# A two-layer hybrid diffusion step on one core: the builder's scheduler orders the instructions by its timeline model

## The chip, the cores and the metric

The kernel runs on one core of one Trainium2 chip. The core's engines are TensorE (PE, matmuls), VectorE (DVE), ScalarE (ACT), GpSimd (POOL) and SyncE (SP, which issues most DMAs). Each takes its own list of instructions strictly in order and waits by semaphores for the others. The metric is the device time of one execution in microseconds (us); lower is better.

## The reference

Two layers over 128 context tokens and 512 latent tokens, D = 1024, in float32; the same weights for both groups, with shifts, scales and gates from each group's conditioning vector.

```
def _layer(x, mod, shared, cached):
    shift1, scale1, gate1, shift2, scale2, gate2 = jnp.split(mod, 6, axis=-1)
    proj = (x * (1 + scale1) + shift1) @ w_in
    ...
    o_rwkv, s_f, s_b = _rwkv_mix(f_rwkv, s0, s0, rwkv_p)
    o_na = _neighbourhood_attention(na_q, na_k, na_v, na_k_ctx, na_v_ctx, rpb)
    ...
    o_g = _blocked_attention(g_q.reshape(b, n, H_GQA_KV, GQA_GROUP, HEAD_DIM), keys, vals)
    ...
    mix = jnp.concatenate([o_rwkv, o_na, o_g], -1) @ w_out
    x = _layer_norm(DEEPNORM_ALPHA * x + gate1 * mix, ln1_w, ln1_b)
    gate, up = jnp.split((x * (1 + scale2) + shift2) @ w_ffn_in, 2, axis=-1)
    x = _layer_norm(DEEPNORM_ALPHA * x + gate2 * ((jax.nn.silu(gate) * up) @ w_ffn_out), ln2_w, ln2_b)
```

`mod` is SiLU(cond) @ w_mod + b_mod. `_rwkv_mix` is a scan over the tokens, forward and backward, in 4 heads of 64 (RWKV-7); the neighbourhood attention has 4 heads on a grid of 8 x 64, with a learned bias; GQA has 8 query and 2 key heads. The outputs are the tokens of both groups, the scan's final states and the context's keys and values.

## The kernel before

The 640 tokens stand in the free dimension, in two halves of 320 columns. Weights arrive as float32 by DMA (`wraw`, L306, two buffers), and `split` makes of each a high and a low part: ACT casts the high one (`whi`, L277), DVE subtracts (`wlo`, L278). `mm3` then issues three matmuls for each block of 128 x 128 (high by high, high by low, low by high). All matmuls pass through one line, L72, transposes through L76, so groups are told apart by their tiles: `ps_s`, `ps_rw` and `ps_pv` are the three kinds of PSUM tiles.

The start (`first_input`) contracts 1024 = 8 x 128 in steps `k`. Each step needs the block `x{k}` of the input (L371) and its scale and shift. These come from `w_modT` (L186, multiplied and summed on DVE, L194) for all scales and for the first two shifts; the other six shifts come from rows of `w_mod` (L203) through matmuls into `ps_pv`, from `cst`, made from `c_raw` through a SiLU (L163). Later modulation values come through `ps_pv` as well.

Each layer has eight jobs of the scan. A job works on chunks of 64 tokens and needs inverses of 64 x 64 triangular matrices: PE's products go to DRAM (`md`), come back as blocks of 16 x 16 (`BT`, L723), DVE inverts the blocks, these go to DRAM (`td`, `xd`, issued by ACT) and come back as 64 x 64 matrices (`T`, L797; `X`, L799), and PE finishes the inverse and forms the states. While a job is between those DMAs, the kernel runs units of the two attentions: keys and queries come from DRAM (`ks`, L962, three buffers; `qs`, L955), the bias (`bias`, L948) and values (`vw`, L938) too. Then follow `w_out`, layer norm (sums `lnS`, `lnQ`), and the feed-forward part.

What sets the order: the program is written as generators. `spawn`, `tick` and `weave` take the next piece of a job when a hand-kept clock (`Tensor.now`, which adds an estimate per matmul) says that it is ready, and so write one sequence. The tile framework's scheduler then goes through it with a model of when each instruction is ready, and appends to each engine's list the ready instruction of the highest priority; priority follows the written sequence, except where `high_priority` moves one (L306's split by 50 places, for example). The model says only in what order instructions are listed; on the chip semaphores decide when they run. Buffers are reused in the listed order, so a load may wait for the last reader of its buffer, and what stands behind it on SP waits too.

The function that the diff touches builds and runs the program:

## Time and profile before

| | |
|---|---|
| median of 3 runs | 2181.78 us (2178.21 to 2183.61) |
| profiled execution, its time | 2182.43 us |
| its span | 2180.7 us, 41209 instructions |
| mean granted clock of PE | 0.965 |
| busy: PE, DVE, ACT, POOL | 94%, 60%, 42%, 9% |
| DMA | 226.46 MB, mean 104 GB/s |

The profile is one execution. Rows of it are times in us from the span's start. PE's matmul and weight loads overlap, and the granted clock is a share of full speed, so a low clock makes matmuls longer without idle time. An idle engine costs nothing by itself: what counts is which wait ends last in each stretch.

### The profile page before, as it was taken

The numbers are of one execution on the slowest core, as the hardware profiler recorded it, in microseconds if no ns is written. First come the engines' busy times: TensorE is split into PE (matmuls) and PEld (weight loads), VectorE is DVE, ScalarE is ACT, GpSimd is POOL, SyncE is SP. The second block draws the span as 40 slices with busy tenths as digits, with TensorE's granted clock in tenths as the row PEclk, the third lists the DMA queues.
The fourth block names the chain that finished last, engine by engine and source line by source line (L and its number), as shares of the span: only waits on it lengthen the run. The fifth ranks groups of instructions, "written<-read, shape, count | busy, mean of one in ns | idle before, by whom it ended". The sixth has DMA issues, their size and how long they took to land.

```text
span 2180.7 us, 41209 instructions
## 1 busy us (share of the span) xinstructions
PE 2052.8 (94%) x16737; PEld 1861.4 (85%) x16737; DVE 1302.1 (60%) x2874; ACT 909.8 (42%) x1823; POOL 189.8 (9%) x355
## 2 busy tenths in 40 slices
PE   6989989799999999999999997879999999999997
PEld 4876867577889999999988886658779999999997
DVE  6445676586776666666765666567767533323247
ACT  3434455465663212212365445356555521221234
POOL 0001131010100000000020223011101000000000
PEclk9999998799999999999999999789999999999998
DMA  8554344211424444444442425241014222222223
GB/s 295 147 161 159 108 94 95 49 34 29 142 73 136 145 155 151 148 139 151 141 133 69 130 69 110 54 94 27 23 48 139 65 69 78 69 73 83 75 84 112
DMA packets 186597, 226.46 MB, mean 104 GB/s; under 512 B 119062, under 2 KB 128918, under 8 KB 186278
## 3 DMA queue, kind: packets, MB, share of 16 engines
q1 hardware_dynamic: 150148, 206.72, 32.3%
q0 software_dynamic: 3984, 11.90, 1.7%
q10 hardware_dynamic: 32274, 5.20, 1.4%
q8 instruction: 132, 2.16, 0.4%
q14 instruction: 59, 0.48, 0.1%
HBM read 198.37 MB, written 25.40 MB: 103 GB/s over the span
## 4 chain that ended last, share of the span: by engine, by line
PE 80%; DMA 8%; DVE 5%; ACT 3%; issue 3%; SPq 1%; POOL 0%; ACTq 0%; DVEq 0%; POOLq 0%
PE ps_s L72 43%; PE ps_rw L72 29%; PE ps_pv L72 5%; PE ps_rw L76 4%; DMA td<-TB 3%; DMA T<-td 1%; DMA wmod<-in_w_mod 1%; ACT whi L277 1%; DMA BT<-md 1%; DVE wlo L278 0%; DMA xa<-in_xT 0%; ACT prob L1127 0%; DMA c_raw<-in_cT 0%; PE ps_s L76 0%; DMA md<-X 0%
## 5 line engine op out<-in xcount | busy, mean ns | idle before, releaser
L72 PE MATMUL ps_s<-xh,whi 128*128 128x320 f32 x1312 | 417.9, 321 | 24.2 <-ACT xh L277 11.6
L72 PE MATMUL ps_s<-xh,wlo 128*128 128x320 f32 x1312 | 409.9, 313 | 2.5 <-DVE wlo L278 2.5
L72 PE MATMUL ps_s<-xl,whi 128*128 128x320 f32 x1312 | 410.0, 313 | 0.6 <-DVE xl L278 0.4
L72 PEld LDWEIGHTS ps_s<-xh,whi 128*128 128x128 f32 x1312 | 249.1, 190 | 46.9 <-ACT xh L277 13.7
L72 PEld LDWEIGHTS ps_s<-xh,wlo 128*128 128x128 f32 x1312 | 249.4, 190 | 6.9 <-DVE wlo L278 4.4
L72 PEld LDWEIGHTS ps_s<-xl,whi 128*128 128x128 f32 x1312 | 249.8, 190 | 5.5 <-issue 2.9
L278 DVE TENSOR_TENSOR wlo<-wraw,whi 128x1024 fp32r<-128x1024 f32 (+1 forms) x118 | 141.4, 1199 | 159.9 <-ACT whi L277 159.2
L72 PE MATMUL ps_s<-xh,flo 128*128 128x320 f32 x736 | 228.7, 311 | 0.0
L72 PE MATMUL ps_s<-xl,fhi 128*128 128x320 f32 x736 | 228.5, 310 | 0.0
L72 PE MATMUL ps_s<-xh,fhi 128*128 128x320 f32 x736 | 228.4, 310 | 0.0
L277 ACT CAST whi<-wraw 128x1024 fp32r<-128x1024 f32 (+1 forms) x118 | 121.1, 1027 | 250.7 <-PE ps_s L72 146.6
L277 ACT CAST fhi<-wraw 128x1024 fp32r<-128x1024 f32 (+1 forms) x82 | 83.3, 1016 | 206.3 <-PE ps_s L72 99.8
L72 PEld LDWEIGHTS ps_s<-xh,fhi 128*128 128x128 f32 x736 | 138.9, 189 | 0.1
L72 PEld LDWEIGHTS ps_s<-xh,flo 128*128 128x128 f32 x736 | 138.8, 189 | 0.1
L72 PEld LDWEIGHTS ps_s<-xl,fhi 128*128 128x128 f32 x736 | 138.9, 189 | 0.0
L278 DVE TENSOR_TENSOR flo<-wraw,fhi 128x1024 fp32r<-128x1024 f32 (+1 forms) x82 | 97.0, 1184 | 57.7 <-ACT fhi L277 57.6
L72 PE MATMUL ps_s<-ks,qs 128*128 128x256 f32 (+1 forms) x384 | 102.4, 373 | 24.9 <-DMA qs<-nqd 15.4
L1431 ACT ACTIVATE sg<-ps_s 128x320 f32<-128x320 f32 x88 | 38.2, 435 | 189.1 <-PE ps_s L72 189.0
L1432 DVE TENSOR_TENSOR sg<-sg,ps_s 128x320 f32<-128x320 f32 x88 | 42.8, 486 | 120.1 <-ACT sg L1431 119.8
L1278 DVE SCALAR_TENSOR_TENSOR z<-ps_rw,modT,z 128x128 f32<-128x128 f32 (+2 forms) x144 | 59.0, 436 | 90.0 <-PE ps_rw L72 89.8
L72 PE MATMUL ps_rw<-hh,flo 128*128 128x320 f32 x352 | 109.7, 312 | 0.6 <-DVE flo L278 0.6
L72 PE MATMUL ps_rw<-hh,fhi 128*128 128x320 f32 x352 | 109.5, 311 | 0.0
(397 smaller groups left out, 4482.1 us busy)
## 6 DMA issues: line engine op xcount, KB each, us to landing
wraw<-in_w_ffn_in SPq DMA_DIRECT2D x88, 512.0 KB
wmod<-in_w_modT SPq DMA_DIRECT2D x66, 512.0 KB
wraw<-in_w_in_f SPq DMA_DIRECT2D x42, 512.0 KB
wraw<-in_w_ffn_out SPq DMA_DIRECT2D x48, 448.0 KB
wmod<-in_w_mod SPq DMA_DIRECT2D x48, 256.0 KB
wraw<-in_w_out SPq DMA_DIRECT2D x16, 512.0 KB
wraw<-in_w_ffn_out SPq DMA_DIRECT2D x16, 512.0 KB
ks<-nkd SPq DMA_DIRECT2D x16, 384.0 KB
```

The costliest lines, as they stand in the source:

```text
L72: self.eng.matmul(out, lhsT, rhs, **kw)
L76: self.eng.transpose(out, src, ident)
L277: self.nc.scalar.copy(hi, src)
L278: self.nc.vector.tensor_tensor(lo, src, self.r32(hi), ALU.subtract)
L1278: nc.vector.scalar_tensor_tensor(z[:, a:b], ps[:, q], g, xa[:, q], ALU.mult, ALU.add)
L1431: nc.scalar.activation(sg, pg, AF.Silu)
L1432: nc.vector.tensor_tensor(sg, sg, pu, ALU.mult)
```

## The change

One argument of the tile framework's context. With it, the scheduler takes its timeline model in place of the default model to decide when instructions are ready, and so which is listed next. Instructions, tiles, buffers and shapes are those of before; there is one table load fewer on ACT.

```
-    with tile.TileContext(nc) as tc:
+    with tile.TileContext(nc, schedule_with_timeline_sim=True) as tc:
         Build(tc, I, O).run()
```

The lists change on all engines. Three places follow; numbers behind a name tell tiles of one kind apart, and names without one are inputs in DRAM if they begin with `in_`.

SP at the start, from the ninth DMA on, before (`wmod` are modulation weights, `x2` to `x7` blocks of the input, `wraw` weights of the projection, `rp` the bias table):

```order
L306 DMA wraw_144<-in_w_in_f 128x1024
L306 DMA wraw_150<-in_w_in_f 128x1024
L186 DMA wmod_163<-in_w_modT 128x1024
L203 DMA wmod_172<-in_w_mod 128x768
L203 DMA wmod_176<-in_w_mod 128x768
L203 DMA wmod_180<-in_w_mod 128x768
L371 DMA x2_186<-in_xT 128x640
L371 DMA x3_248<-in_xT 128x640
L203 DMA wmod_184<-in_w_mod 128x768
```

And now:

```order
L186 DMA wmod_163<-in_w_modT 128x1024
L203 DMA wmod_172<-in_w_mod 128x768
L371 DMA x2_186<-in_xT 128x640
L371 DMA x3_248<-in_xT 128x640
L371 DMA x4_284<-in_xT 128x640
L371 DMA x5_337<-in_xT 128x640
L371 DMA x6_376<-in_xT 128x640
L371 DMA x7_415<-in_xT 128x640
L203 DMA wmod_602<-in_w_mod 128x512
L306 DMA wraw_144<-in_w_in_f 128x1024
L203 DMA wmod_618<-in_w_mod 128x512
L916 DMA rp_1052<-in_rpb 60x31
```

All blocks of the input and `wmod_602` moved ahead of `wraw_144`, and the rows `wmod_176` to `wmod_184` behind `rp_1052`.

ACT near the end of the scan's feature stage, before (`cx`, `f`, `rt`, `FT`, `BK` and `RHO` are features of the scan; `whi_1131` is the high part of the attention's first query weights):

```order
L524 COPY cx_960<-ps_s2_927 128x320
L670 ACTIVATE rt30_1204<-rt30_1204 128x320
L528 ACTIVATE f8_995<-cx_960,pp0_103 128x512
L672 ACTIVATE rt00_1225<-rt20_1173 128x320
L673 ACTIVATE rt20_1173<-rt20_1173 128x320
L535 ACTIVATE rt10_1172<-ps_rw_1178,hbias_1068 128x320
L535 ACTIVATE f8_995<-f8_995 128x640
L732 COPY RHO0_1492<-FT0_1222 128x320
L684 COPY BK0_1223<-BK0_1223 64x5x64
L277 CAST whi_1131<-wraw_1133 128x1024
L277 CAST whi_1234<-wraw_1236 128x1024
L988 ACTIVATE nqc_1125<-ps_s2_1137 128x128
```

And now, the place at which `whi_1131` stands:

```order
L210 COPY wmod_784<-ps_pv_601 64x256
L277 CAST whi_921<-wraw_923 128x1024
L524 COPY cx_786<-ps_s2_757 128x320
L528 ACTIVATE f4_829<-cx_786,pp0_103 128x512
L277 CAST whi_1131<-wraw_1133 128x1024
L524 COPY cx_875<-ps_s2_842 128x320
L562 ACTIVATE kksq_1085<-kk1_1083 128x640
L678 COPY FT0_1222<-f4_829 128x5x64
L678 COPY FT1_1786<-f4_829 128x5x64
L528 ACTIVATE f5_914<-cx_875,pp0_103 128x512
```

The cast moved from behind the features' decay and key tiles to a place ahead of `cx_875`, 22 rows up.

SP in layer 1, at the second pair of heads of the neighbourhood attention, before (`nkd1`, `nqd1` hold its keys and queries, `gkd1`, `gqd1` those of GQA, `md` a product of the scan):

```order
L962 DMA ks_15155<-nkd1_12541 64x2x768 x2
L955 DMA qs_15161<-nqd1_12540 128x1x512
L955 DMA qs_15163<-nqd1_12540 128x1x512
L723 DMA BT1_14794<-md_14632 40x16x16
L962 DMA ks_15158<-nkd1_12541 64x2x768
L948 DMA bias_15128<-rpx1_12473 128x8x32 x4
L948 DMA bias_15137<-rpx1_12473 128x8x32 x4
```

And now:

```order
L962 DMA ks_15155<-nkd1_12541 64x2x768 x2
L955 DMA qs_15161<-nqd1_12540 128x1x512
L955 DMA qs_15163<-nqd1_12540 128x1x512
L962 DMA ks_15158<-nkd1_12541 64x2x768 x2
L723 DMA BT1_14794<-md_14632 40x16x16
L948 DMA bias_15128<-rpx1_12473 128x8x32 x4
L955 DMA qs_15599<-gqd1_12902 128x1x512
L962 DMA ks_15596<-gkd1_12903 64x2x768 x2
L955 DMA qs_15601<-gqd1_12902 128x1x512
```

Both halves of `ks_15158` moved ahead of `BT1_14794`, and the first loads of GQA ahead of the second bias.

## Rows read from the trace of the kernel before

**Rows 1.** The page, part 1: busy us of the engines.

```profile
PE 2052.8 (94%) x16737; PEld 1861.4 (85%) x16737; DVE 1302.1 (60%) x2874; ACT 909.8 (42%) x1823; POOL 189.8 (9%) x355
```

**Rows 2.** The page, part 4: the chain that ended last, by engine.

```profile
PE 80%; DMA 8%; DVE 5%; ACT 3%; issue 3%; SPq 1%; POOL 0%; ACTq 0%; DVEq 0%; POOLq 0%
```

**Rows 3.** What PE waited for, whole span: us in total, times, longest.

```profile
PE ps_rw L72 <- DMA T<-td: 24.0, 6, 10.1
PE ps_s L72 <- DMA qs<-nqd: 15.4, 2, 11.1
...
PE ps_s L72 <- ACT whi L277: 7.9, 6, 3.7
PE ps_pv L72 <- DMA wmod<-in_w_mod: 5.8, 8, 1.3
PE ps_s L72 <- DMA qs<-gqd: 5.3, 2, 4.2
...
PE ps_s L72 <- DVE lnQ L1291: 2.3, 1, 2.3
...
PE ps_pv L72 <- issue: 1.2, 1, 1.2
```

**Rows 4.** Windows: busy us (x count) by engine; clock, DMA share, GB/s.

```profile
8.00:12.00 4.00, 3.71 (x5) 0.98 (x3) 0.92 (x8) 0.00 (x1) 0.61 (x1) 1.00 1.04 385
12.00:16.00 4.00, 0.00 (x0) 0.00 (x0) 3.12 (x5) 3.93 (x5) 0.00 (x0) 1.00 0.56 189
16.00:20.00 4.00, 0.00 (x0) 0.00 (x0) 4.00 (x7) 1.54 (x2) 0.00 (x0) 1.00 0.82 285
...
125.00:130.00 5.00, 4.64 (x18) 4.24 (x19) 2.08 (x2) 0.64 (x1) 0.00 (x0) 0.55 0.55 166
130.00:135.00 5.00, 5.00 (x34) 4.19 (x33) 0.36 (x1) 0.49 (x2) 0.00 (x0) 1.00 0.45 150
650.00:700.00 50.00, 50.00 (x343) 50.00 (x342) 32.20 (x54) 23.28 (x42) 0.00 (x0) 1.00 0.37 117
1350.00:1400.00 50.00, 29.07 (x305) 22.40 (x304) 21.47 (x79) 16.09 (x49) 5.71 (x9) 0.72 0.32 76
```

**Rows 5.** SP's DMA issues, 0 to 30 us: start, us, and what.

```profile
14.43 2.67 SPq L306 DMA_DIRECT2D wraw<-in_w_in_f  x2
```

**Rows 6.** The chain, start of the kernel: start, us, and what.

```profile
3.14 8.83 DMA c_raw<-in_cT
...
17.63 6.51 DMA wmod<-in_w_mod
...
27.83 5.95 DMA wmod<-in_w_mod
```

**Rows 7.** The chain, 110 to 132 us.

```profile
123.65 1.05 ACT whi L277
...
126.01 5.08 PE ps_s L72 x22
```

**Rows 8.** SP's DMA issues, 360 to 382 us.

```profile
369.91 0.30 SPq L723 DMA_DIRECT2D BT<-md  x1
...
376.65 1.68 SPq L955 DMA_DIRECT2D qs<-gqd  x2
```

**Rows 9.** The chain, 370 to 415 us.

```profile
388.59 16.65 DMA td<-TB
...
405.30 5.27 DMA T<-td
```

**Rows 10.** The chain, 1390 to 1480 us.

```profile
1419.17 5.67 DMA td<-TB
...
1452.50 15.28 DMA td<-TB
```

**Rows 11.** SP's DMA issues, 1388 to 1416 us.

```profile
1396.01 0.31 SPq L723 DMA_DIRECT2D BT<-md  x1
1410.01 0.62 SPq L962 DMA_DIRECT2D ks<-nkd  x1
```

## The prediction, made before the changed kernel was run

> **What bounds the kernel now.** I read the page's busy times first: TensorE (PE) is busy 94% of the span [rows 1], and the chain that ended last is 80% PE [rows 2]. The other 20% is what an order can change. Next the windows: one of 50 us in layer 0's feed-forward part has 50.00 us of PE and a granted clock of 1.00 [rows 4]. The order of PE's matmuls in the two such stretches (about 650 to 1050 us and 1690 to 2150 us) is the same in both kernels, so four tenths of the span cannot move. The place of worst use is 1350 to 1400 us: 29.07 us of PE at a clock of 0.72 [rows 4]. Third, PE's waits name what there is to win [rows 3]: the scan's T tile, read back from DRAM (24.0 us, 6 times); the queries qs of the neighbourhood attention (15.4 us, twice); the weight splits whi (7.9 us, 6 times); modulation weights (5.8 us, 8 times); the queries of GQA (5.3 us, twice); and lnQ between the layers (2.3 us). That is 60.7 us. Last, the chain at single places tells whether an earlier issue would shorten a wait.
>
> **The change.** No instruction's work changes; each engine runs its list strictly in order, and the lists change. I cost the places at which an instruction that is waited for moves.
>
> *Start.* SP now issues x2 to x7 and wmod_602 ahead of wraw_144, and cos, sin, wmod_618, wraw_584 and wraw_668 ahead of later rows of w_mod. By their shapes, x4 to x7 are 4 x 0.33 MB, the two wmod 2 x 0.26, cos and sin 2 x 0.26 and the two wraw 2 x 0.52: 3.4 MB ahead of the last w_mod row. At 385 GB/s, the rate at 8 to 12 us [rows 4], that is 8.8 us. Against it stands time in which the DMA engines were not full: SP stood at wraw_144 until 14.43 us [rows 5], and the share was 0.56 at 12 to 16 and 0.82 at 16 to 20 [rows 4], so 1.8 + 0.7 = 2.5 us can be filled. These rows matter: the chain at the start runs through c_raw (8.83 us) and two waits for w_mod (6.51 and 5.95 us) [rows 6]. The whole amount of data before 60 us is nearly the same, and the third and later steps of the contraction find their x earlier; so the bounds are -2.5 and +8.8 and I take **+3**, near the middle, since a late third step is partly made up by quicker later ones.
>
> *Near 120 us.* ACT's cast whi_1131 stood behind 22 rows, most of the scan's features, and PE waited for it: ACT began it at 123.65, VectorE (DVE) made wlo from it, and PE went on at 126.01 [rows 7]. Of the 7.9 us, the longest piece is 3.7 [rows 3]. Afterwards the clock was low: at 125 to 130 us 18 matmuls at 0.55 against 34 in the next 5 us at 1.00 [rows 4], so (34 - 18) / 34 x 5 = 2.4 us went there. In the new order the cast stands 22 rows earlier on ACT, its load ahead of waiting wmod loads on SP. Bounds: 0 (another split, whi_1234, is late in its stead) and -(1.2 + 3.7 + 2.4) = -7.3, where 1.2 is the one wait of ps_pv for issue just before [rows 3]. I take **-6**, by the nearest end, since the cast needs nothing that comes late.
>
> *Modulation waits.* 5.8 us in 8 pieces [rows 3]; their matmuls move behind other PE work. Between 0 and -5.8: **-2**.
>
> *Scores of layer 0.* The shorter of the two waits for qs of the neighbourhood attention is 15.4 - 11.1 = 4.3 us [rows 3]; the loads behind it now go ahead of a BT load that waited for md. The longer one, in layer 1, keeps its order on SP: 0. Between 0 and -4.3: **-2**.
>
> *GQA's first loads.* ks_4382 and qs_4385 were issued behind BT0_3880 (369.91) and eight vw loads, qs_4385 at 376.65 [rows 8]; they now stand ahead of these. The 5.3 us of waits for them should go. But the next wait, for T0_4275, is set by td<-TB (16.65 us from 388.59) and T<-td (5.27 us) [rows 9], and the product ahead of it isn't earlier. So most is given back, unless the transfer gets quicker because fewer loads run beside it: the same transfer took 5.67 us in layer 1 [rows 10], 11.0 less. Bounds 0 and -11.0; I take **-3**, nearer to 0, because two loads of keys (ks_5400) still run beside it.
>
> *Between the layers.* PE now has some 7 us of matmuls ahead of its wait for lnQ, which is 2.3 us [rows 3]: **-2**, from bounds of 0 and -2.3.
>
> *New waits on SP.* Seven BT loads of the inverse now stand behind loads of keys or queries that need a buffer. The nearest row: at BT1_14794 the load was issued at 1396.01 and the second half of ks behind it at 1410.01 [rows 11]. In the new order both halves of ks come first. Were PE's last reader of that buffer as late as before, BT would be held 14.0 us. PE's four matmuls for ps_s2_14930 on ks_14157 now run as one piece, some 40 to 60 rows earlier in PE's list, so the buffer should be free before md lands. Bounds 0 and +14.0: **+2**, nearer to 0.
>
> Everything else I cost at nothing: DVE and ACT have idle time (60% and 42% busy [rows 1]) that covers their small shifts; if one of them were late at a hand-over to PE, each would cost about its own instruction, as the 1.05 us of a cast [rows 7].
>
> Sum: 3 - 6 - 2 - 2 - 3 - 2 + 2 = **-10 us**, against 2182.4 us of the profiled execution: 2172.4. The median of the three runs is 0.65 us lower, so I say **2172**. About 0.3%, 6.5 us, is what a measurement can tell from no change.
>
> **Rivals.**
>
> A, *slower: SP stands in front of BT*. Place: the BT loads above. It decides if the buffer of ks is released later than md lands. At BT1_14794 it costs 14.0 us, and 2.4 us at the low clock behind the stall, 16.4 in place of 2; the gains of -2 and -3 at score loads don't come, for the same reason. 3 - 6 - 2 - 2 + 16.4 = +9.4: about **2192**. For it: a wait for md stands ahead of most of these loads in SP's list, and T is PE's largest wait [rows 3]. Against it: the reader of ks is earlier. The Trainium skill, DMA: Bandwidth & Descriptors, section Anatomy of one DMA, says that a semaphore wait is done by the issuing sequencer and that DMA engines themselves don't wait; by that rule every load behind a waiting one waits too, and the rows of SP agree (no issue between 1396.01 and 1410.01 [rows 11]).
>
> B, *no change: paid back*. Each stall that is filled returns at the next wait for T (six waits, 24.0 us [rows 3]), because td<-TB sets the pace (15.28 us in layer 1 too [rows 10]). Then the places near 120 us and at the start and a little of the rest are left: 3 - 6 + 2 = -1, **2181**. For it: PE's work between the last product and the first use of T is nearly as much as before. Against it: five of the terms lie away from T.
>
> C, *no change: the start costs its full price*. The late rows of w_mod hold PE for the whole 8.8 us: -10 - 3 + 8.8 = -4.2, **2178**. This is the case of loads that are taken strictly in the order of issue. The Trainium skill, DMA: Bandwidth & Descriptors, section Queues, rings and completion order, says that each DMA engine takes a ring's descriptors in ring order, which speaks against moving x4 to x7 forward; the rate of 385 GB/s at the start [rows 4] shows no room for both.
>
> D, *more gain*. td<-TB runs free at 389 us (-11.0 in place of -3), the place at 120 us gives -7.3, the start 0: -10 - 8 - 1.3 - 3 = -22, **2160**.
>
> That the change does nothing is excluded by the lists, which differ on all engines.
>
> **Numbers.** Forecast 0.38, A 0.26, B 0.16, C 0.10, D 0.10. Faster by over 0.3% (under 2175.2): forecast and D, 0.48. Within: B and C, 0.26. Slower (over 2188.3): A, 0.26. The range reaches upward to A with the start at its full price (2192 + 5.8, so 2198) and down to D with all of the 5.8 us of the modulation waits (2160 - 3.8, so 2156): **2156 to 2198**. About 2 in 10 lie beyond its two ends, where several bounds would have to come together, or a place that I cost at nothing decides. The forecast's own range is 2165 to 2179, from half of each bound.
>
> **What would show it.** Right: PE without the wait for whi near 120 us; no wait for qs of GQA near 390; waits for T still some 20 us; 1350 to 1400 us as poor as before. A: SP idle in front of ks_15158, BT1_14794 issued later than md's landing, and a longer T<-td wait. C: PE's third step of the contraction later than 40 us by 6 or more. Wrong altogether: waits of PE at a place that I cost at nothing, as scores that now run in one group behind a late qs, or split weights that come late in the feed-forward part.

## The result, and the profile after

The changed kernel takes **2241.5 us** (median of 4 runs, 2239.2 to 2248.9) against 2182.7 us before: a ratio of 1.0277, 95% interval 1.0259 to 1.0295. It is 2.8% slower; the forecast was 2172, with a range that ended at 2198. The profiled execution has a span of 2241.3 us and a mean granted clock of 0.950, where before had 2180.7 and 0.965.

The page's busy times of the changed kernel, against [rows 1]:

```profile
PE 2074.1 (93%) x16737; PEld 1886.3 (84%) x16737; DVE 1298.8 (58%) x2874; ACT 903.2 (40%) x1822; POOL 179.1 (8%) x355
```

TensorE (PE) runs the same 16737 matmuls and is busy 21.3 us longer, at a lower mean clock. The other part of the 60.6 us of span is waiting. What PE waited for, whole span, against [rows 3] (us in total, times, longest):

```profile
PE ps_s L72 <- ACT xh L277: 14.8, 9, 4.6
PE ps_s L72 <- DMA qs<-nqd: 13.3, 1, 13.3
PE ps_rw L76 <- DVE XB L779: 11.0, 1, 11.0
PE ps_s L72 <- issue: 8.6, 1, 8.6
...
PE ps_rw L72 <- DMA T<-td: 5.1, 2, 5.0
...
PE ps_rw L76 <- DVE RV L744: 4.0, 2, 3.8
...
PE ps_s L72 <- ACT whi L277: 2.9, 3, 1.3
...
PE ps_pv L72 <- DMA wmod<-in_w_mod: 2.3, 4, 1.0
```

The waits that the forecast went for did shrink: T from 24.0 to 5.1, wmod from 5.8 to 2.3, whi from 7.9 to 2.9 in the rows with ps_s (beside a new wait of 3.9 for whi with ps_rw), and qs<-gqd from 5.3 to nothing. All of PE's waits for a DMA, summed over this view, fell from 50.5 us (18 times) to 20.7 (7 times). But its waits for ACT and VectorE (DVE) rose from 60.3 us (74 times) to 120.4 (119 times), and one wait of 8.6 us "for issue" has no releaser in the trace (below). In all, 116.5 us became 153.8. The waits' 37.3 us and the 21.3 us of busy time make 58.6 of the 60.6 us.

To see where, I take the start of the n-th matmul of PE in both traces (their number is the same) and call the difference the lag. By the time in the kernel before, the lag is +0.7 us at 116, -9.4 at 288, +21.1 at 378, +3.4 at 435, +33.3 at 725 and +33.9 through the feed-forward part to 1050; then +29.3 at 1223, +46.2 at 1442, +32.9 at 1492, +60.9 at 1748, and +59.8 at the end. So the kernel gains 10 us before 288 us. At the scores of layer 0 it loses 30.5 and regains 17.7, at those of layer 1 it loses 16.9 and regains 13.3. And it loses **29.9 us between 435 and 725** and **28.0 between 1492 and 1748**. These two stretches are the last heads of a layer's attention, the output projections and the start of the feed-forward part; the forecast has no term in either. Two executions of the same lists can stand 2 us apart in this count: late0_only, a run below that keeps the old lists up to 450 us, has -2.2 at 71 us.

Windows of the changed kernel at the places that the forecast spoke of, against [rows 4] (us, busy us and count of PE, its weight loads, DVE, ACT and POOL; clock, DMA share, GB/s):

```profile
12.00:16.00 4.00, 0.00 (x0) 0.00 (x0) 3.04 (x5) 2.89 (x4) 0.00 (x0) 1.00 1.02 401
16.00:20.00 4.00, 1.49 (x4) 0.19 (x4) 4.00 (x8) 0.68 (x2) 0.00 (x0) 1.00 1.04 397
...
125.00:130.00 5.00, 5.00 (x35) 4.40 (x35) 0.72 (x2) 0.71 (x4) 0.00 (x0) 1.00 0.29 78
...
300.00:350.00 50.00, 29.14 (x258) 20.92 (x257) 19.79 (x77) 14.04 (x46) 2.68 (x5) 0.67 0.34 76
```

The DMA engines are now full at 12 to 20 us and the low clock near 125 us is gone. The scores of layer 0 (300 to 350 us) got worse: before, the same window had

```profile
300.00:350.00 50.00, 40.48 (x370) 29.31 (x370) 32.05 (x117) 22.49 (x70) 10.29 (x16) 0.76 0.43 93
```

**The late stretch** shows best what happened. Four windows of 40 us, the kernel before:

```profile
440.00:480.00 40.00, 39.37 (x467) 31.27 (x462) 31.84 (x81) 25.02 (x54) 6.39 (x9) 1.00 0.15 35
480.00:520.00 40.00, 39.48 (x478) 31.40 (x477) 27.98 (x73) 20.89 (x45) 4.71 (x6) 1.00 0.12 26
520.00:560.00 40.00, 39.06 (x515) 31.36 (x514) 28.40 (x78) 22.84 (x45) 0.39 (x2) 1.00 0.14 38
560.00:600.00 40.00, 38.53 (x349) 35.82 (x346) 29.99 (x63) 24.18 (x41) 5.82 (x11) 1.00 0.56 181
```

and the changed kernel:

```profile
440.00:480.00 40.00, 36.89 (x421) 28.92 (x417) 30.77 (x76) 23.20 (x50) 5.92 (x9) 1.00 0.15 36
480.00:520.00 40.00, 36.76 (x410) 29.10 (x412) 25.87 (x68) 18.49 (x39) 3.00 (x4) 0.91 0.08 18
520.00:560.00 40.00, 38.23 (x475) 30.54 (x469) 27.89 (x78) 21.54 (x46) 2.09 (x4) 1.00 0.16 40
560.00:600.00 40.00, 33.98 (x394) 28.93 (x394) 20.81 (x53) 16.03 (x36) 1.68 (x3) 0.86 0.19 64
```

Before, PE is busy 156.4 of these 160 us at a clock of 1.00, and DVE is busy three quarters of the time beside it. After, it is 145.9, and the clock falls twice. PE's timeline at these two places (start, length, instruction, and in brackets the idle time ahead of it and who ended it):

```profile
482.33 1.03 PE L76 MATMUL ps_rw<-ident,prob 128*128 128x128 f32 x6 [3.78 <-DVE RV L744]
...
579.87 0.33 PE L72 MATMUL ps_rw<-S,A 64*64 64x64 f32 x4 [2.05 <-ACT o L1142]
580.72 0.42 PE L72 MATMUL ps_s<-xh,whi 128*128 128x320 f32 x1 [0.52 <-ACT whi L277]
```

and the windows around the second:

```profile
575.00:585.00 10.00, 6.25 (x66) 4.70 (x62) 9.93 (x24) 7.43 (x18) 0.00 (x0) 0.84 0.12 35
585.00:590.00 5.00, 5.00 (x39) 4.81 (x40) 0.69 (x4) 0.00 (x0) 0.00 (x0) 0.63 0.40 143
595.00:600.00 5.00, 4.33 (x26) 3.82 (x26) 1.88 (x5) 0.92 (x3) 0.00 (x0) 0.55 0.57 194
```

From 575 to 585 us DVE is busy 9.93 of 10 us, ACT 7.43 and PE 6.25. That DVE is full is not what is new. At the same work the kernel before had

```profile
565.00:575.00 10.00, 8.53 (x76) 6.64 (x77) 9.33 (x23) 7.67 (x16) 1.69 (x3) 1.00 0.47 134
```

with PE at 8.53 and a clock of 1.00. New is what stands in front. ACT casts ten blocks `xh` of the attention's output in one run, and DVE subtracts ten of the twelve `xl` in one run; the output projection, which uses them one by one, begins only at 580.72 us. Before, DVE did the twelve as 3, 1, 1 and 7, with the scan's small steps and the split of the first weights between them:

```profile
574.09 3.69 ACT L277 CAST xh<-o 128x320 fp32r<-128x320 f32 x10
575.09 4.26 DVE L278 TENSOR_TENSOR xl<-o,xh 128x320 fp32r<-128x320 f32 x10
```

ACT's copy of `o`, for which PE waits 2.05 us, begins at 579.14, behind 13 such casts. In the five us after 585, DVE has 0.69 us of work. Seven waits at 575 to 600 us are 5.5 us together, and the clock behind them is 0.63 and 0.55, which by these two rows costs some 4 us more (0.37 x 5.00 + 0.45 x 4.33).

At the start of the feed-forward part PE's first matmul stands right behind the transposes of the layer norm's values, where before 13 (layer 0) and 99 (layer 1) other matmuls lay between. PE, and DVE's two groups ahead of it:

```profile
645.43 0.64 PE L72 MATMUL ps_s<-xh,whi 128*128 128x320 f32 x1 [4.56 <-ACT xh L277]
```

```profile
640.21 3.30 DVE L1329 TENSOR_TENSOR z<-z,lnm 128x320 f32<-128x320 f32 x8 [0.32 <-ACT lnm L1316]
643.44 3.29 DVE L1330 TENSOR_TENSOR z<-z,lnr 128x320 f32<-128x320 f32 x8
```

DVE takes all eight tiles of z through its first step, 3.3 us, before the first tile's second step begins, and ACT's xmod and xh of that tile come only behind it. It does the second step of all eight in another 3.3 us before it goes on to other work. Before, it took four tiles at a time (1.70 us) and then alternated the rest with other work.

### The profile page after: what moved, and what is told of

Read it like the earlier page. It is cut to its first block, busy times and chain, and to the rows that moved or that the text cites. A ratio compares the mean times of both kernels' runs of the same rounds, so it can differ in the third digit from the quotient of the medians.

```text
span 2241.3 us, 41237 instructions
## 1 busy us (share of the span) xinstructions
PE 2074.1 (93%) x16737; PEld 1886.3 (84%) x16737; DVE 1298.8 (58%) x2874; ACT 903.2 (40%) x1822; POOL 179.1 (8%) x355
## 5 line engine op out<-in xcount | busy, mean ns | idle before, releaser
L72 PE MATMUL ps_s<-xl,whi 128*128 128x320 f32 x1312 | 418.7, 319 | 4.2 <-DVE xl L278 3.6
L72 PE MATMUL ps_s<-xh,wlo 128*128 128x320 f32 x1312 | 417.5, 319 | 1.4 <-DVE wlo L278 1.4
L72 PEld LDWEIGHTS ps_s<-xh,whi 128*128 128x128 f32 x1312 | 255.1, 195 | 45.2 <-ACT xh L277 19.0
L72 PEld LDWEIGHTS ps_s<-xl,whi 128*128 128x128 f32 x1312 | 255.5, 195 | 11.8 <-DVE xl L278 6.9
L72 PEld LDWEIGHTS ps_s<-xh,wlo 128*128 128x128 f32 x1312 | 255.6, 195 | 5.6 <-DVE wlo L278 2.8
L194 DVE CUSTOM_DVE_ANT_0 modx<-wmod,c_rows,pp 128x1024 bf16<-128x1024 f32 x66 | 84.5, 1283 | 125.6 <-DMA wmod<-in_w_modT 124.6
L72 PE MATMUL ps_s<-ks,qs 128*128 128x256 f32 (+1 forms) x384 | 92.2, 365 | 28.3 <-DMA qs<-nqd 13.3
L76 PE MATMUL ps_rw<-ident,prob 128*128 128x128 f32 x536 | 93.6, 299 | 21.9 <-DVE XB L779 11.0
L72 PE MATMUL ps_rw<-hl,fhi 128*128 128x320 f32 x352 | 109.0, 310 | 0.0
L72 PE MATMUL ps_rw<-hh,whi 128*128 128x320 f32 x352 | 108.7, 309 | 0.3 <-ACT hh L277 0.3
```

The lines of the kernel that those rows point to most:

```text
L72: self.eng.matmul(out, lhsT, rhs, **kw)
L76: self.eng.transpose(out, src, ident)
L194: nc.vector.tensor_tensor_reduce(o, w, c[:, i], 1.0, self.par(l, "b_mod", j), ALU.mult, ALU.add, self.modT[l][:, j, i:i + 1])
```

## The experiments

The first four ask which engine, the next five where in time, and the others what happens at one place. The method is the same in each: the flag stays on, and behind the builder's run a helper adds edges along a stored list of instruction numbers. Such an edge fixes the order of issue on an engine and waits for nothing:

```
+def pin(tc, nc, names=PINNED):
+    by = {i.name: i for i in nc.cur_bb.bb.instructions}
+    info = mybir.DependencyInfo(mybir.DependencyClass.NoSync, mybir.DependencyReason.DATA)
...
+            for a, b in zip(seq, seq[1:]):
+                tc.add_manual_dep(by[b], a, info, reason="pin")
...
         Build(tc, I, O).run()
+        pin(tc, nc)
```

`PINNED` names the engines, the pieces of the list, and the list. The scheduler places whatever isn't pinned.

**One engine's old list, the other engines free.**

```
+PINNED = {"PE": (0, None, list of before)}     # or DVE, SP, ACT
```

> The new scheduler, but PE's list is held to the order of before (edges that order the issue and wait for nothing); all other engines are listed by the timeline model. Theory P (PE's own list is the cost: scores and transposes stand ahead of ready work and wait for loads): 2185 to 2205 us, and the wait for qs near 319 and the stretches after 435 and 1490 us recover. Theory S (SP's list is the cost, loads of keys ahead of BT): 2225 to 2245. Theory D (DVE's list, the inverse ahead of softmax): 2215 to 2235.

> The new scheduler, with DVE's list held to the order of before. Theory D: 2190 to 2210 us, DVE's waits for BT fall from 41.0 us to under 10, and PE's wait of 11.0 us for XB goes. Theory P: 2225 to 2240, since only that one wait and a few of 3 to 5 us go. Theory S: 2235 to 2245.

> The new scheduler, with SP's list (all its DMA issues) held to the order of before. Theory S: 2185 to 2205 us, BT issued when md has landed, and the waits at 319, 340 and 1402 us smaller. Theories P and D: 2235 to 2255, since PE and DVE stand at the same places; the gain of 10 us near 120 us may be lost too, as wraw_1133 is behind waiting wmod loads again.

> The new scheduler, with ACT's list held to the order of before. All three theories: 2235 to 2260 us, no recovery; the cast whi_1131 is late again near 120 us and the 10 us won there go, so 2250 is likeliest. A fourth theory (ACT's list is the cost): under 2215.

Measured: PE 2271.5 us (ratio 1.0411, 1.0389 to 1.0433), DVE 2273.4 (1.0416, 1.0398 to 1.0435), SP 2258.9 (1.0353, 1.0325 to 1.0381), ACT 2312.6 (1.06, 1.0576 to 1.0624). All miss, and all are slower than the changed kernel itself. An old list among new ones doesn't give back that engine's part; it adds waits, as the largest of the kernel with ACT's old list show:

```profile
PE ps_pv L72 <- DMA wmod<-in_w_mod: 20.4, 9, 9.7
PE ps_rw L72 <- DMA X<-xd: 16.6, 1, 16.6
```

No guilty engine was found this way: each old list among four new ones was worse than all new ones. So the next runs hold all engines, by stretches of time.

**Regions.** In each, all five lists of the named stretch (by the time of before) are those of before, or the other way round.

```
+PINNED = {"PE": ([(1438, None)], ...), "DVE": ([(339, None)], ...), ...}   # tail_before: from 280 us on
+PINNED = {"PE": ([(1438, 4220)], ...), "DVE": ([(339, 1119)], ...), ...}   # mix0_before: 280 to 720 us
+PINNED = {"PE": ([(2370, 4220)], ...), "DVE": ([(694, 1119)], ...), ...}   # late0_before: 450 to 720 us
+PINNED = {"PE": ([(0, 2370), (4220, None)], ...), ...}                     # late0_only: all but 450 to 720 us
+PINNED = {"PE": ([(1438, 6498), (7499, None)], ...), ...}                  # hybrid: all but 0 to 280 and 1054 to 1223 us
```

> The new scheduler up to 280 us of before's time; behind that all five engines keep before's lists. Theory R (each region's loss or gain is its own): the 10 us won near 120 us stay and nothing is lost later: 2173, within 2168 to 2178. Theory B (paid back at a later wait): 2179 to 2186.

> The new scheduler everywhere, but all five engines keep before's lists from 280 to 720 us of before's time (layer 0's scan, attentions and the beginning of its feed-forward part). Theory R: the 44 us that this region lost come back: 2197, within 2190 to 2205. If the region's loss comes from loads that its neighbours moved: above 2215.

> The new scheduler everywhere, but all five engines keep before's lists from 450 to 720 us of before's time only: the late jobs of the scan, GQA, the output projection and the beginning of the feed-forward part of layer 0. Theory R: of the 42 us that mix0_before won, 30 come from this stretch, in which PE waits hardly for DMAs but for ACT and DVE: 2211, within 2205 to 2217. Theory E (the early stretch with its waits for loads is the cost): 2225 or more.

> The reverse of late0_before: before's lists everywhere, the new scheduler's only from 450 to 720 us of before's time. Theory N (the new lists of this stretch are worse by themselves): 2183 + 30 = 2213, within 2207 to 2219. Theory U (the stretch only continues what went wrong upstream): 2180 to 2192.

> The new scheduler where it won (up to 280 us, and from 1054 to 1223 us of before's time, around the change of layers), before's lists elsewhere. Theory R: 2183 - 10 - 4 = 2169, within 2164 to 2174, faster than both kernels. Theory B: 2177 to 2186.

Measured:

| kernel | median, us | ratio to before | interval |
|---|---|---|---|
| tail_before | 2174.7 | 0.9963 | 0.9949 to 0.9977 |
| mix0_before | 2199.2 | 1.0074 | 1.0059 to 1.0089 |
| late0_before | 2210.1 | 1.0128 | 1.0101 to 1.0155 |
| late0_only | 2211.9 | 1.0145 | 1.0130 to 1.0160 |
| hybrid | 2173.5 | 0.9955 | 0.9941 to 0.9968 |

All five came out as the theory said that gives each region its own loss or gain. The new order is worth about -8 us up to 280 us (tail_before), and the stretch of 450 to 720 us costs 31 us whether it is taken out of the changed kernel (2241.5 - 2210.1) or put alone into the old one (2211.9 - 2180.6, the kernel before beside it), and the old lists from 280 to 450 us as well give another 11 (2210.1 - 2199.2). What lies behind 720 us costs some 24 us in all (2199.2 of mix0_before less 2174.7 of tail_before). Only the stretch of 450 to 720 us was tried both ways; the other numbers are differences of neighbouring runs. The **hybrid**, new lists where they gain and old ones elsewhere, is faster than both kernels: 2173.5 us, 0.45% below before (its interval ends at 0.9968). From tail_before, which keeps the old lists at 1054 to 1223 us too, it can't be told apart. Its largest waits:

```profile
PE ps_rw L72 <- DMA T<-td: 24.2, 5, 10.1
PE ps_s L72 <- DMA qs<-nqd: 11.2, 1, 11.2
```

It keeps the old waits for T, and PE's waits for ACT and DVE are 61.7 us in all, as before the change (60.3).

**The scores of layer 0.** SP's transfers, PE and DVE in the changed kernel:

```profile
314.52 8.06 SPq L955 DMA_DIRECT2D qs<-nqd  x2
329.47 0.31 SPq L723 DMA_DIRECT2D BT<-md  x1
```

```profile
319.27 1.19 PE L72 MATMUL ps_s<-ks,qs 128*128 128x256 f32 x4 [8.57 <-issue]
...
340.38 0.47 PE L76 MATMUL ps_rw<-ident,prob 128*128 128x128 f32 x1 [10.96 <-DVE XB L779]
```

```profile
339.38 0.16 DVE L775 COPY XB<-BT 40x2 f32<-40x2 f32 x1 [11.24 <-DMA BT<-md]
```

PE stands 8.6 us at a group of scores, of which the trace names no releaser (the load of its queries is likely: half of the packets of these two loads had run by 317.6 us). Then DVE stands 11.2 us at BT, a load of 40 KB for the scan's triangular inverse, with the copies that PE needs behind it. The two waits hang together. The products of FT and BK from which BT's data is made stand behind the scores in PE's list; so ACT stores `md` only at 321.94 us, and SP waits for it:

```profile
320.39 1.22 PE L72 MATMUL ps_rw<-FT,BK 64*128 64x128 f32 x4
```

```profile
SPq L723 <- DMA md<-X: 6.8, 1, 6.8
```

Two edits of the changed lists: the group of four score matmuls behind a few products of FT and BK and one transpose, and the first five DVE instructions of the inverse behind the copies; and in a second kernel also BT ahead of the keys and queries on SP.

```
 PE   ... FT,BK products, transpose of prob
+PE   ps_s2_3510<-ks_3000,qs_3006 x4          (was ahead of them)
 DVE  ... T0_3434, OT, two copies of pT
+DVE  XB1<-BT1_3386, first 5                  (was ahead of them)
+SP   BT1_3386<-md                            (second kernel only)
 SP   ks_3962 x2, qs_3968, qs_3970
-SP   BT1_3386<-md                            (second kernel only)
```

> All lists are those of the changed kernel, except two places near 310 to 340 us: PE's four score matmuls on ks_3000 and qs_3006 stand behind the product and the transpose that were behind them, and DVE's first five instructions of the inverse of BT1_3386 stand behind four that PE and others wait for. Theory H (a single instruction that is listed ahead of its load holds ready work): PE's waits of 8.6 and 11.0 us shrink to under 4 each, and the time falls by 10 to 20 us, to 2222 to 2232. Theory B (what is won is paid back at the next wait for T): 2236 to 2242.

> The kernel of local_moves, and on SP the load BT1_3386 stands again ahead of the two loads of ks_3962 and the loads qs_3968 and qs_3970. Theory Q (transfers queued ahead of BT make it late): BT lands some 11 us after its issue in place of 16, near 333, PE's wait of 10.1 us near 339 falls to 4 to 6, and the place at 353 us of the changed kernel is reached 9 to 12 us earlier in place of 5.5. The whole: 2230 to 2240, as part may return in layer 1. Theory W (BT's time to land is its own): no change against local_moves.

Measured: 2242.3 us (1.0263, 1.0244 to 1.0282) and **2230.9 us** (1.0218, 1.0193 to 1.0243). The first edit alone did nothing for the time: PE's wait at the scores is 6.8 us, and that of 11.0 us became one of 10.2, with another name. SP came to BT 8.0 us earlier (321.49 for 329.47), but its issue took 6.37 us there, and BT was used only 1.8 us earlier:

```profile
321.49 6.37 SPq L723 DMA_DIRECT2D BT<-md  x1
```

```profile
337.62 0.16 DVE L775 COPY XB<-BT 40x2 f32<-40x2 f32 x1 [10.55 <-DMA BT<-md]
```

In the second kernel it goes out ahead of the queries:

```profile
316.88 0.31 SPq L723 DMA_DIRECT2D BT<-md  x1
317.24 1.87 SPq L962 DMA_DIRECT2D ks<-nkd  x2
319.15 4.25 SPq L955 DMA_DIRECT2D qs<-nqd  x2
```

```profile
325.94 0.15 DVE L775 COPY XB<-BT 40x2 f32<-40x2 f32 x1
```

From the start of the issue to first use it is 9.1 us here and 16.1 in the first kernel, with nothing else changed, and no wait for it is left. PE passes the place 17 us earlier than in the changed kernel, of which 10.6 us stay to the end. So two things are shown: the edits on PE and DVE are worth nothing alone, and with BT ahead of the loads on SP 10.6 us. BT's move on SP was not tried alone; in the changed kernel `md` has not landed before 329.4 us, so there BT ahead of the queries would have held them.

**The start of the feed-forward part.** The first three matmuls behind 24 of the output projection, in both layers; and in a second kernel DVE also alternates its z groups with the evacuations that PE's projection waits for.

```
+PE   24 x ps_rw<-xh,hh / xl,hh / xh,hl       (were behind)
 PE   ps_s2_7211<-xh_6589,whi / xl_6590,whi / xh_6589,wlo
```

> All lists are those of the changed kernel, but on PE, at the first block of each layer's feed-forward part, its three first matmuls stand behind 24 matmuls of the output projection that were listed right behind them and were ready. Theory H (a consumer listed without cover behind its producers; behind it nothing is waited for but PE's own work, so nothing is paid back): of the two waits of 4.6 + 1.1 us, the 3.6 us of the 24 matmuls are covered in each layer, and 1 to 2 us of low clock: 8 to 12 us in all, 2231 within 2227 to 2235. Theory B (paid back): 2238 to 2244.

> The kernel of ffn_moves, and on DVE, at the layer norm ahead of each feed-forward part, the eight subtractions and eight multiplications of z no longer stand in one run of 6.6 us: they alternate tile by tile, with the two evacuations of the output projection (z from ps_rw) among them. Theory V (the place is held by DVE's list and by PE's at once; either alone moves the wait to the other): the wait of 6.4 and 6.8 us for the evacuation falls to under 2 and no wait for xh comes in its stead; with the low clock behind it, 5 to 7 us in each layer: 2230, within 2225 to 2234. Theory L (the layer norm's chain itself is too long to hide): 2238 to 2245.

Measured: 2243.5 us (1.0278, 1.0248 to 1.0309) and 2240.0 (1.0274, 1.0253 to 1.0295). No gain from the first: the wait for xh became one for the evacuation of the projection's buffers, which DVE does behind the same two groups:

```profile
PE ps_rw L72 <- DVE z L1278: 16.3, 4, 6.8
```

In the second these waits fell to 3.1 us in layer 0, and the median can't tell 2240.0 from 2241.5. So in the first kernel moving PE's instructions only renamed the wait, and in the second the waits shrank without a gain that the median shows. Inconclusive as to the price of this place.

**The stretch of 450 to 590 us.** First all engines, then the transfers alone, PE and DVE alone, and the last part alone:

```
+PINNED = {"PE": [(2370, 3391)], "DVE": [(694, 951)], "ACT": [(460, 611)], "SP": [(256, 280)], "POOL": [(147, 172)]}  # late0a_before
+PINNED = {"SP": [(256, 280)], "POOL": [(147, 172)]}                                                                  # late0a_sp
+PINNED = {"PE": [(2370, 3391)], "DVE": [(694, 951)]}                                                                 # late0a_pe_dve
+PINNED = {"PE": [(2927, 3391)], "DVE": [(841, 951)], "ACT": [(542, 611)], "SP": [(266, 280)], "POOL": [(161, 172)]}  # late0end_before: 525 to 590 us
```

> The new scheduler everywhere, before's lists only from 450 to 590 us of before's time (the late jobs of the scan and GQA). By the time at which PE starts the same count of matmuls in both traces, 20 of the 30 us are lost here and 10 from 590 to 720 (output projection, layer norm, begin of the feed-forward part): 2221, within 2216 to 2227. If the two halves depend on each other: above 2230 or under 2214.

> Changed kernel; only SP's and POOL's lists of 450 to 590 us are those of before (one BT load one place earlier on SP, 12 rows on POOL), and PE, DVE and ACT keep the changed lists everywhere. Theory C (the 26 us that late0a_before gained lie in the orders of PE, DVE and ACT): 2241 us, 2236 to 2246. Theory Q (they lie in the order of the transfers): about 2215 us, 2210 to 2222.

> Changed kernel; only PE's and DVE's lists of 450 to 590 us are those of before, ACT, SP and POOL are left to the scheduler and come out nearly as in before there. Theory V (the two lists that hand over to each other carry the 26 us, ACT's order follows from them): 2215 us, 2209 to 2222. Theory W (ACT's own order is a part of it): between 2222 and 2241 us, or above 2241 if the lists no longer fit together.

> Changed kernel; only the lists of 525 to 590 us of before (all engines: the last part of layer 0's attention and the first products behind it) are those of before. In the changed kernel TensorE waits 5.5 us at 575 to 600 us and then runs at clocks of 0.55 to 0.76, about 6 us more. Theory E (the pile-up of VectorE's and ScalarE's work at 575 to 585 us is made by the order of this last part): 10 of the 26 us that the longer piece gained come back, 2231 us, 2226 to 2236, and the clock at 560 to 600 us is 0.95 or more. Theory F (it is made by what was left over from 450 to 525 us): 2241 us, 2236 to 2246, with the waits at its place as before the edit.

Measured: 2215.4 us (1.0163, 1.0146 to 1.0180), 2240.3 (1.0272, 1.0251 to 1.0294), 2226.0 (1.0203, 1.0186 to 1.0220) and 2232.6 (1.0229, 1.0201 to 1.0256). All engines' old lists in this stretch give back 26 us, more than forecast. In the lag of the profiled executions the stretch itself gives back 19.4 us, all that was lost between 450 and 590; where the rest arises isn't shown. The windows are then those of before:

```profile
440.00:480.00 40.00, 39.61 (x482) 31.69 (x480) 32.10 (x83) 25.10 (x56) 6.38 (x9) 1.00 0.14 31
480.00:520.00 40.00, 39.77 (x481) 31.54 (x479) 28.36 (x72) 20.99 (x45) 4.69 (x6) 1.00 0.12 25
520.00:560.00 40.00, 38.16 (x511) 30.88 (x511) 27.44 (x77) 22.59 (x44) 0.39 (x2) 1.00 0.14 38
560.00:600.00 40.00, 38.18 (x341) 34.98 (x337) 28.14 (x60) 22.72 (x40) 5.26 (x10) 1.00 0.54 175
```

The transfers alone give back nothing that the median shows, so the loss lies in the orders of PE, DVE and ACT. PE and DVE alone give 15 of the 26 us, which is within the range of theory W (ACT's own order is a part). The last part alone gives 9 us, as theory E said, DVE's twelve subtractions stand again as 3, 1, 1 and 7, and the clock at 560 to 600 us is back at 1.00:

```profile
560.00:600.00 40.00, 37.31 (x445) 32.44 (x445) 27.21 (x64) 20.98 (x42) 3.20 (x6) 1.00 0.39 128
```

So the pile-up at 575 to 585 us is made by the order of this last part, not carried into it, and it is one of several losses in the stretch.

**The wait at 482 us.** The changed lists, with the first eight (layer 0) and ten (layer 1) DVE instructions of an inverse moved behind the copies that PE needs:

```
 DVE  ... copies of RV and pT that PE waits for
+DVE  XB<-BT0_5104, first 8; XB<-BT1_15901, first 10    (were ahead of them)
```

> All lists are those of the changed kernel, except on DVE near 480 and 1532 us: the first eight and ten instructions of the inverse of BT0_5104 and BT1_15901 stand behind the next copies and sums that PE waits for. Theory D (DVE stands for BT in front of copies that PE needs): PE's waits of 3.8 us at each place go, with the low clock of the next 10 us (0.66 there): 5 to 7 us at each, 2229, within 2225 to 2234. Theory B (paid back at a later wait): 2237 to 2244.

Measured: 2240.7 us (1.0270, 1.0252 to 1.0288). The wait of 3.8 us went and the place at 514 us was reached 3.7 us earlier (a clock of 0.66 at 490 to 495 us came even so), but by 831 us 1.4 were left, and at the end of the span nothing. In late0a_sp too the wait fell (to 0.4 us, with BT one place earlier on SP), the same place was 4.9 us earlier, 4.0 at 832, and nothing was left at the end. So in two runs without this wait no gain shows at the end.

## Why the prediction was wrong

The step that failed is the sentence "Everything else I cost at nothing: DVE and ACT have idle time (60% and 42% busy [rows 1]) that covers their small shifts; if one of them were late at a hand-over to PE, each would cost about its own instruction". It is an average, where the order within a stretch decides. At 575 to 585 us ACT and DVE work through ten blocks for the output projection, in front of what PE waits for; at 640 us DVE works on eight tiles of z while PE stands for the first of them. A late hand-over cost more than the producer's own instruction, namely all that stood in front of it (2.05 us for a copy of 0.58), and matmuls behind the waits at 482 and 580 us ran at a clock of 0.53 to 0.63. And there were not one or two hand-overs: PE's waits for ACT and DVE went from 74 to 119. Their 60.1 us more, less the 29.8 us of DMA waits saved, with 7.4 more for issue and the 21.3 of slower matmuls, make 59.0 of the 60.6 us.

By its own terms:
- *Start*, +3: the lag is +2.1 us at 71 us and +0.7 at 116, which is no more than one execution differs from another. The idle DMA engines of [rows 4] were filled (shares of 1.02 and 1.04), and the late rows of w_mod cost little. Right in that rival C, the full price of 8.8, did not come; the +3 itself can't be told from nothing.
- *Near 120 us*, -6, and *modulation waits*, -2: together -10.0 between 116 and 168 us. Right in cause (no wait for whi there, a clock of 1.00 at 125 to 130 us), 2 us too small.
- *Scores of layer 0*, -2: about **+22** between 288 and 341 us. Wrong in sign. The forecast counted only what the loads of queries gain by going ahead of BT. Against it stood PE's 8.6 us at the scores, which kept `md` back, and the 11 us that DVE, and PE behind it, stood for BT; local_moves_sp got 10.6 us of it back by the orders on PE, DVE and SP together.
- *GQA's first loads*, -3: the three waits of 4.24, 1.07 and 7.43 us for qs and T are gone, and between 378 and 435 us the lag falls by 17.7, more than the bound of -11.0. It follows a loss of 30.5 (from 288 to 378 us), of which it gives back a part; that T's transfer had run on while PE stood near 340 us is argued, not shown. The forecast also had waits for T stay at some 20 us; they fell to 5.1.
- *Between the layers*, -2: -4.6 from 1050 to 1223 us. Right in sign on the spot; in the medians it doesn't show (2173.5 of the hybrid, 2174.7 of tail_before).
- *New waits on SP*, +2: at the place that it was costed by, SP waited 22.0 us in front of ks_15158, but `md` was stored only at 1430.59 us and BT1_14794 issued at 1432.93, so the wait held nothing. In layer 1 the lag rises to +46.2 at 1442 us and is back at +32.9 by 1492.
- *Nothing elsewhere*, 0: **+29.9** and **+28.0** in the two late stretches. late0_only shows the first by itself: 31 us. The second was not tried by itself; the medians say that all behind 720 us costs some 24 us, its gains counted in.

Of the rivals, A had the right sign and the right tile (BT behind ks and qs), but another mechanism and a sixth of the size: not SP idle in front of a full buffer, but a transfer that runs behind others, and DVE in line behind it. The rule cited with C is the Trainium skill's, DMA: Bandwidth & Descriptors, section Queues, rings and completion order: each DMA engine takes a ring's descriptors in order. The trace agrees at BT, which was used 16.1 us after its issue behind two loads of queries and 9.1 us ahead of them; at the start the order cost nothing that could be told. B's pay-back is seen with the other sign: at 435 and 1492 us a part of a loss is regained, where PE waited for T before. The last sentence of the prediction named waits "at a place that I cost at nothing" and the scores behind a late qs as what would prove it wrong, and both happened; it gave them no chance of their own.

What stays open: how the 26 us of 450 to 590 us split further. 9 us are the last part, PE with DVE hold 15, the wait at 482 us is some 4 to 5 on the spot; that the rest is ACT's order follows from a difference of two runs and was not tried alone. What the stretch of 590 to 720 us loses (10 us by the lag, 5.3 by the medians of late0a_before and late0_before) and the late stretch of layer 1 were not taken apart.

## What to carry to other kernels

When an instruction order changes, count the hand-overs between engines in both lists, place by place, and ask at each what still stands in front of the producer's instruction. Shares of busy time don't answer this, neither over the span nor in a window: DVE was as good as full at the same work in both kernels, 9.33 and 9.93 of 10 us. Here an order that loads earlier saved 29.8 us of DMA waits and lost twice that in waits on VectorE and ScalarE, and behind several of these TensorE ran at its low clock. Orders can be taken apart by stretch with edges that wait for nothing, and the best one may be a mixture: the one stretch that was tried both ways cost the same in either surroundings, while no engine's list could be exchanged alone.

## What the runs showed that I had not expected

A load of 40 KB took at least 7 us longer because of its place on the queue alone (16.1 and 9.1 us from issue to first use, local_moves and local_moves_sp; in the second nothing waited for it). The packets of the trace show how. While the last two loads of queries ran (326 to 338 us of the changed kernel) the DMA share is mostly 0.13, two of 16 engines, and the rate mostly 43 to 51 GB/s, against about 400 at 12 to 20 us. Of BT's 640 packets of 64 bytes, 512 ran at 330.4 to 331.0 us and the last 128 at 337.5 to 339.1, as the queries ended (338.6); in local_moves it is 328.5 to 329.2 and 335.5 to 337.3, the queries ending at 336.8. That this last fifth is the share of the two busy engines is an inference; the trace doesn't name a packet's engine.

A wait of 3.78 us was followed by five us at the low clock. The windows from 480 us on, in the changed kernel:

```profile
480.00:485.00 5.00, 2.41 (x27) 1.91 (x28) 4.39 (x17) 1.57 (x3) 0.00 (x0) 0.79 0.13 49
485.00:490.00 5.00, 5.00 (x28) 3.91 (x30) 3.69 (x7) 1.92 (x4) 0.00 (x0) 0.53 0.00 0
490.00:495.00 5.00, 4.54 (x54) 3.40 (x51) 4.38 (x11) 2.31 (x8) 0.24 (x1) 1.00 0.08 8
```

28 matmuls in five us at 0.53, near 1.2 of 2.4 GHz, are half of what PE does here at 1.00: the stall costs some 2.4 us (an estimate: 0.47 of five) after it is over, beside its own 3.78. It needn't be one long wait: in bt_moves, where no wait there is over 1.3 us, PE was busy 3.21 of the five us from 485 on, and the clock of the next five was 0.66.

And the lists depend on each other: any one of four old lists (PE, DVE, SP, ACT) among the new ones cost 17 to 71 us more than all new ones.
